# Sample's late products with cached keys, tied behind levels of linear attention, with their sums one step later

## The chip, the core and the metric

The program runs on one core of a Trainium2 chip. The metric is device time in microseconds of one execution, compared by the median of several. A core has a matmul engine (TensorE, in the profile PE; its weight loads are PEld), VectorE (DVE), ScalarE (ACT), GpSimd (POOL) and SyncE (SP), which here issues nearly all DMAs. Each engine works off its own queue in the order in which the program was built; an instruction that waits holds up all that stand behind it in its queue.

## What is computed

One inference step of a hybrid decoder layer, for a prompt of 2048 positions and for eight samples of eight new positions each. One projection is split into dilated sliding-window attention (8 heads of 64), gated linear attention (4 heads, key size 64, value size 128) and gates; both results are gated and go through one output projection.

```python
def reference(x_prompt, x_sample, cache_k_win, cache_v_win, state_gla, norm_w, w_in, ...):
    ...
        hp, kp, vp, st_p = mixer_layer(hp, pos_p, attend_prompt, s0, *params)
        att_s = functools.partial(attend_sample, cache_k_win[layer], cache_v_win[layer])
        hs, kn, vn, st_s = mixer_layer(hs, pos_s, att_s, state_gla[layer], *params)

def mixer_layer(x, pos, attend, s0, ...):
    z = rmsnorm(x, norm_w) @ w_in
    q, k, v, qb, kb, vb, g_lr, gate_a, gate_b = jnp.split(z, split_points(), axis=-1)
    ...
    o_a = attend(q, k, v)
    log_a = jax.nn.log_sigmoid(g_lr @ w_gate_up + b_gate) / GATE_TAU
    o_b, s_fin = gla_chunked(qb * DK_B ** -0.5, kb, vb, log_a, s0)
    ...

def dilated_branch_sample(q, k_buf, v_buf, window, dil):
    ...
    s = jnp.einsum('bthd,btnhd->bthn', q, kg) * (hd ** -0.5)
```

The change concerns the last line, the scores of a sample's queries with its cached keys, for the last two of the eight samples.

## The kernel before

The program is written out in full by Python code and put in order by a scheduler that keeps, on each engine, close to the order in which the code is written. Four phases follow each other: the first projections (q, k, v) with the prompt's first attention branches; the rest of the prompt's attention, woven with the projections of the linear attention's queries and keys; from about 736 us the prompt's linear attention, woven with the gate and value projections (`acc_g`, `acc_vb`, later `acc_gb`); and from about 1100 us the sample's attention with the output projection (`Y`).

**Linear attention** (class `gla_core`, `gla_prompt`) runs over eight blocks of 256 positions, called e0 to e7, each of two chunks of 128. Within a block the decays between positions are covered by seven levels, B = 1, 2, 4, ... 64. From the gates' projection `u` come `la` and, by a scan on VectorE, the running sums `b` (L223). Then for each level `front` (L229 on) forms on POOL the difference `D` (L236), on ScalarE its exponential `E` (L244, three instructions, two buffers), and on VectorE the scaled keys `ks` (L249) and queries `qbd` (L252). Two levels later `back` multiplies them on TensorE (`sc`, L280, and L266 for the last level) and VectorE copies the result by a mask into `Ac` (L286). In the first levels of a block the block before it is finished: `kd` on POOL, its transpose `ptk` (L323) copied by VectorE to `kdt` (L325), and in `chunk` the state update `U` (L1266), the output `O` (L1274, L1280) and the new state `Sbd` (L1287). The `U` of the second chunk reuses a buffer that the first chunk's `Sbd` reads.

**Products with cached keys** are steps of one sample b and one t of 0 to 7. `sample_keys` loads the query row, broadcast to all partitions (`qb`), and 128 keys of the branch with dilation 16 (`k3`), and for t under 4 those with dilation 4 (`k2`, used for t and t + 4). In the next step `sample_scores` calls `dot` twice: POOL multiplies (`pr`, L964), VectorE sums over each head (L965) into `sck`. The buffer `pr` is single, so POOL can begin a product only when VectorE has summed the one before. After t = 7 a DMA writes the scores out. The samples 0 to 5 are done beside the attention; samples 6 and 7, 16 steps with 32 products, stay for the third phase (`late_dots`).

**The weave** takes generators with a number of steps each and always advances the one whose share done is lowest. In the third phase these are the projections, the linear attention (74 steps, the first 15 empty), the fetch of a weight, and `late_dots` (33 steps: 15 empty, 17, and one). A generator may answer `WAIT`, and then the next is tried. What is left goes into a second weave with the sample's own linear attention (`sample_gla`), which begins when `late_dots` is done.

Of the kernel before, what the change touches and what calls it, by code (L numbers as in the profile page):

```python
# [7 lines left out]
F32 = mybir.dt.float32  # L8
# [5 lines left out]
ALU = mybir.AluOpType  # L14
# [4 lines left out]
P = 128  # L19
# [33 lines left out]
def tile_hymba(ctx: ExitStack, tc: tile.TileContext, A: dict):  # L53
    nc = tc.nc
    PE, ACT, DVE, POOL, SP = nc.tensor, nc.scalar, nc.vector, nc.gpsimd, nc.sync
# [87 lines left out]
    class gla_core:  # L143
# [85 lines left out]
        def front(self, li):  # L229
            gt, st, n, B = self.pools[1], self.st, self.n, self.levels[li]  # L230
            halves = lambda f: f.rearrange("p (m two B) -> p m two B", two=2, B=B)
            M = n // B
            bv = halves(self.b[:].rearrange("p a c -> p (a c)"))
            D = gt.tile([P, 2 * n], F32, name=f"D_{self.tagp}_{B}", tag="D", bufs=2)
            dv = halves(D[:])
            POOL.tensor_tensor(  # L236
                dv, bv, bv[:, :, 0:1, B - 1 : B].to_broadcast([P, M, 2, B]), ALU.subtract
            )
            E = st["E"][li % 2]
            ev = E[:, :, :n].rearrange("p i (m B) -> p i m B", B=B)  # L240
            for i, (rows, half) in enumerate(
                ((slice(0, P), 0), (slice(0, 64), 1), (slice(64, P), 1))
            ):
                ACT.activation(  # L244
                    ev[rows, i], dv[rows, :, half, :], AF.Exp, scale=(2 * half - 1) / 16.0
                )
            ks, qbd = st["ks"][li % 3], st["qbd"][li % 3]
            kv, qv = (halves(f.rearrange("p a c -> p (a c)")) for f in (self.kT, self.qT))
            DVE.tensor_tensor(  # L249
                halves(ks[:, : 2 * n])[:, :, 0, :], kv[:, :, 0, :], ev[:, 0], ALU.mult  # L250
            )
            DVE.tensor_tensor(  # L252
                qbd[:, :, :n].rearrange("p i (m B) -> p i m B", B=B),
                qv[:, :, 1, :].unsqueeze(1).to_broadcast([P, 2, M, B]), ev[:, 1:3], ALU.mult,
            )

        def back(self, li):
            st, n, C, nch, B = self.st, self.n, self.C, self.nch, self.levels[li]
# [96 lines left out]
    WAIT = object()  # L355
# [25 lines left out]
    with ExitStack() as c1:  # L381
# [579 lines left out]
        def dot(out, kt, qt, tag):  # L961
            sk = sk_state["pool"]
            pr = sk.tile([P, 512], F32, name=f"pr_{tag}", tag="pr", bufs=1)
            POOL.tensor_tensor(pr[:], kt, qt, ALU.mult)  # L964
            DVE.tensor_reduce(  # L965
                out, pr[:].rearrange("p (u k d) -> p u k d", u=2, k=4), AX.X, ALU.add
            )

        def sample_keys(b, t):
            sk = sk_state["pool"]  # L970
            qt = sk_state["q", t] = sk.tile([P, 512], F32, name=f"qb_{b}_{t}", tag="qbc")
            SP.dma_start(qt[:], q_s[8 * b + t : 8 * b + t + 1, :].to_broadcast([P, 512]))
            k3 = sk_state["k3", t] = sk.tile([P, 512], F32, name=f"k3_{b}_{t}", tag="k3")
            SP.dma_start(k3[:], ck[b].rearrange("(m r) c -> r m c", r=16)[t])
            if t < 4:
                k2 = sk_state["k2", t] = sk.tile([P, 512], F32, name=f"k2_{b}_{t}", tag="k2")
                SP.dma_start(k2[:], ck[b, W - 512 : W, :].rearrange("(j r) c -> r j c", r=4)[t])

        def sample_scores(b, t):
            if t == 0:  # L980
                sk_state["sc"] = sk_state["pool"].tile(
                    [P, 2, 64], F32, name=f"sck_{b}", tag="sc"
                )
            sc = sk_state["sc"]
            out = sc[:].rearrange("p g (u t k) -> p g t u k", u=2, t=8)[:, :, t]
            qt = sk_state["q", t]
            dot(out[:, 1], sk_state["k3", t][:], qt[:], f"3_{b}_{t}")
            dot(out[:, 0], sk_state["k2", t % 4][:], qt[:], f"2_{b}_{t}")
            if t == 7:
                SP.dma_start(sc_d[b * P : (b + 1) * P, :], sc[:].rearrange("p g c -> p (g c)"))  # L990

        def scores_of(batches):
            todo = [(b, t) for b in batches for t in (0, 4, 1, 5, 2, 6, 3, 7)]

            def step(i):
                if i < len(todo):
                    sample_keys(*todo[i])
                if i:
                    sample_scores(*todo[i - 1])

            return [lambda i=i: step(i) for i in range(len(todo) + 1)]
# [463 lines left out]
        c_sk = ExitStack()  # L1465

        def late_dots():
            for _ in range(15):
                yield
            sk_state["pool"] = c_sk.enter_context(  # L1470
                tc.tile_pool(name="sk3", bufs=2, reuse_waits="tile")
            )
            for f in scores_of(range(6, 8)):
                f()
                yield
            c_sk.close()
            mixed.add("dots")
# [3 lines left out]
                yield  # L1481

        gla_all = [chain(beginning(), gla_prompt()), 74]
        late = [late_dots(), 33]
        host = [rest("g", "vb"), steps("g") + steps("vb")]
        fetch = [load_w("gb"), 2 * KT + 1]
        left = weave(host, gla_all, fetch, late, until=[host, fetch])
# [506 lines left out]
```

## Time and profile before

| what | value |
|---|---|
| median of 3 runs | 1349.1 us |
| lowest and highest | 1347.7 and 1352.2 us |
| the profiled execution | 1350.2 us |
| its span, first to last instruction | 1348.4 us |
| mean granted clock of TensorE | 0.975 |
| DVE busy, 736 to 872 us and 872 to 957 us | 117.7 of 136 us and 52.9 of 85 us |
| POOL busy in the same | 100.6 and 44.8 us |
| PE busy in the same | 120.4 and 83.2 us |

A row of a group or of the timeline gives the line in the kernel, the engine, the operation, and what it writes and reads; the bracket behind a row of the timeline is the time for which the engine stood idle before it, and what ended that. Buffer and block numbers are left out of the names (`D_e` is `D` of any block). A busy TensorE may still run slowly: the granted clock is 1.00 or 0.50 in each slot.

### The profile page before, as it was taken

Reading aid. Unit: us, or ns where it says so; the run is one execution under the profiler, and the core shown is the slowest. Engines: PE = TensorE matmul, PEld = TensorE weight load, DVE = VectorE, ACT = ScalarE, POOL = GpSimd, SP = SyncE. Lnnn points to the kernel's source line nnn. Section 1 sums busy time; section 2 is a strip of 40 time slices with the busy share of each in tenths; the row PEclk is TensorE's granted clock in tenths of the full one; section 3 lists DMA queues with packets and bytes.
Section 4 is the critical chain, followed back from the end, with each engine's and each line's share of the span. In section 5 each row is a group of like instructions: output and inputs, shape, how many; then the busy total and the mean of one; then the engine's idle time right before and its main releaser. Section 6 shows DMA issues by size and latency. Waiting matters only on the chain.

```text
span 1348.4 us, 26203 instructions
## 1 busy us (share of the span) xinstructions
PE 1217.5 (90%) x8878; PEld 727.7 (54%) x8878; DVE 926.2 (69%) x2275; ACT 877.7 (65%) x2332; POOL 634.4 (47%) x598
## 2 busy tenths in 40 slices
PE   3797999888899889997989789999999979999998
PEld 1343565555566555676667556666554434444443
DVE  6366767788677966767665988755673388878741
ACT  5655787678568776878886656566764375556520
POOL 0086553778678645651114876744462133332310
PEclk9998999999999899999999999999999989999999
DMA  8859857767956699968986457543227579998752
GB/s 257 244 172 261 227 155 162 202 202 222 237 168 204 182 273 274 304 209 198 219 194 195 131 173 231 171 126 97 91 94 221 185 240 354 332 378 306 288 208 78
DMA packets 251800, 285.27 MB, mean 212 GB/s; under 512 B 125441, under 2 KB 160338, under 8 KB 251666
## 3 DMA queue, kind: packets, MB, share of 16 engines
q1 hardware_dynamic: 251666, 283.60, 70.0%
q8 instruction: 70, 1.15, 0.3%
q14 instruction: 64, 0.52, 0.1%
HBM read 183.12 MB, written 75.24 MB: 192 GB/s over the span
## 4 chain that ended last, share of the span: by engine, by line
PE 36%; DVE 17%; DMA 13%; POOL 12%; issue 12%; ACT 9%; SPq 2%; POOLq 0%; DVEq 0%; ACTq 0%
PE acc_qkb L1118 5%; PE Y L1616 4%; PE acc_g L1118 3%; PE acc_vb L1118 3%; POOL pr L964 3%; DVE qbd L252 3%; PE O L476 3%; PE s L443 3%; PE t L461 2%; PE acc_gb L1118 2%; DMA T_q<-qp_d 2%; PE acc_v L1118 2%; PE acc_k L1118 2%; PE acc_q L1118 2%; POOL pt L428 2%
## 5 line engine op out<-in xcount | busy, mean ns | idle before, releaser
L1118 PEld LDWEIGHTS <-hr 128*128 128x128 f16 x1824 | 175.3, 99 | 132.0 <-issue 14.0
L964 POOL TENSOR_TENSOR pr<-k,qb 128x512 f32<-128x512 f32 x128 | 177.0, 1383 | 117.3 <-DVE sck L965 80.8
L1118 PEld LDWEIGHTS <-hl 128*128 128x128 f16 x1248 | 122.1, 100 | 153.0 <-issue 25.3
L454 ACT ACTIVATE p<-p,o 128x256 f32<-128x256 f32 (+1 forms) x384 | 173.3, 455 | 45.7 <-DVE o L451 41.8
L1616 PE MATMUL Y<-w_o,mh 128*128 128x512 f16 x768 | 177.5, 381 | 3.6 <-ACT mh L1575 3.5
L428 POOL TENSOR_TENSOR pt<-p,pt 128x512 f16<-128x512 f32 (+1 forms) x80 | 94.7, 1184 | 158.6 <-ACT pt L427 137.9
L476 PE MATMUL O<-v,pt 128*128 128x128 f16 x1200 | 110.4, 221 | 27.0 <-POOL pt L428 8.7
L965 DVE TENSOR_REDUCE sck<-pr 128x8 f32<-128x512 f32 x128 | 87.1, 681 | 58.8 <-POOL pr L964 58.5
L1616 PEld LDWEIGHTS <-mh 128*128 128x128 f16 x768 | 71.9, 98 | 90.5 <-issue 8.7
L461 PE MATMUL t<-ident,p 128*128 128x128 f32 x600 | 106.2, 281 | 7.4 <-ACT p L454 3.0
L476 PEld LDWEIGHTS <-pt 128*128 128x128 f16 x1200 | 82.0, 98 | 51.8 <-POOL pt L428 14.1
L1658 POOL TENSOR_TENSOR tc<-oc,w 128x512 f32<-128x512 f32 x32 | 44.4, 1407 | 138.8 <-DVE w L1650 115.6
L1118 PE MATMUL acc_g<-w_g,hr 128*128 128x272 f16 (+1 forms) x768 | 104.0, 283 | 0.0
L1118 PE MATMUL acc_v<-w_v,hl 128*128 128x512 f16 x384 | 93.8, 388 | 8.3 <-DVE za L798 3.2
L244 ACT ACTIVATE E<-D_e 128x256 f32<-128x256 f32 x168 | 67.3, 418 | 49.3 <-POOL D_e L236 20.5
L1118 PE MATMUL acc_q<-w_q,hl 128*128 128x512 f16 x384 | 93.5, 393 | 5.6 <-ACT zs_k L676 4.2
L451 DVE CUSTOM_DVE_ANT_0 p<-s,m3w,scl_s 128x128 f32<-128x128 f32 (+1 forms) x256 | 89.0, 395 | 10.4 <-PE s L443 5.0
L1118 PE MATMUL acc_k<-w_k,hl 128*128 128x512 f16 x384 | 89.9, 379 | 2.1 <-ACT zs_k L676 1.6
L1118 PE MATMUL acc_vb<-w_vb,hr 128*128 128x512 f16 x384 | 90.8, 385 | 0.0
L443 PE MATMUL s<-kk,qq 128*128 128x256 f16 (+1 forms) x512 | 82.7, 273 | 6.9 <-DMA kk<-kp_d 3.6
L1118 PE MATMUL acc_gb<-w_gb,hr 128*128 128x512 f16 x384 | 87.1, 380 | 0.0
L461 PEld LDWEIGHTS t<-ident,p 128*128 128x128 f32 x600 | 68.4, 143 | 18.2 <-ACT p L454 7.7
(509 smaller groups left out, 2600.5 us busy)
## 6 DMA issues: line engine op xcount, KB each, us to landing
k<-in_cache_k_win SPq DMA_DIRECT2D x104, 256.0 KB
sv<-in_cache_v_win SPq DMA_DIRECT2D x24, 1024.0 KB
hr<-h_d SPq DMA_DIRECT2D x44, 512.0 KB
qb<-q_d SPq DMA_DIRECT2D x64, 256.0 KB
o_d<-o SPq DMA_DIRECT2D x96, 132.0 KB
oc<-o_d SPq DMA_DIRECT2D x48, 264.0 KB
x<-in_x_prompt SPq DMA_DIRECT2D x16, 512.0 KB
h_d<-hl SPq DMA_DIRECT2D x16, 512.0 KB
```

The costliest lines, as they stand in the source:

```text
L244: ACT.activation(ev[rows, i], dv[rows, :, half, :], AF.Exp, scale=(2 * half - 1) / 16.0)
L428: POOL.tensor_tensor(l, f, h, ALU.subtract)
L443: PE.matmul(s_ps[:, i * w : (i + 1) * w], q, k, start=(n == 0), stop=(n == len(prods) - 1),)
L451: DVE.tensor_tensor_reduce(s[:, sl], s_ps[:, sl], mask, neg, BIG, ALU.add, ALU.min, nmf(i))
L454: ACT.activation(s[:, sl], s[:, sl], AF.Exp, bias=nmf(i), scale=-1.0, accum_out=denf(i))
L461: PE.transpose(p_ps[:, i * P : (i + 1) * P], t["s"][:, i * P : (i + 1) * P], ident[:])
L476: PE.matmul(o_, t["pt"][:, c, (i * nb + b) * P : (i * nb + b + 1) * P], vf(i, b), start=(n == 0), stop=(n == 2 * nb - 1),)
L964: POOL.tensor_tensor(pr[:], kt, qt, ALU.mult)
L965: DVE.tensor_reduce(out, pr[:].rearrange("p (u k d) -> p u k d", u=2, k=4), AX.X, ALU.add)
L1118: PE.matmul(z, a_[:, k, :], w[:, p_, k, cols], start=(k == 0 and i == 0), stop=(k == KT - 1 and i == 2),)
L1616: PE.matmul(Y[:], a_[:, k, :], w_[:, part, k, :512], start=(i == 0), stop=(i == len(prods) - 1),)
L1658: eng.tensor_tensor(t_[:], oc[:, g, :, 0:64], w[:, g].unsqueeze(2).to_broadcast([P, NH, HD]), ALU.mult,)
```

## The change

`front` now keeps its `D` instruction and its `qbd` instruction in `st["pins"]`. `late_dots` starts after 6 empty steps and has 18 working steps in a weave of 25, so that it advances once for about three levels. In each step the sums of the step before last's keys, the loads of the next keys and the products of the last keys are issued, in this order, inside `tc.issue_after` for both pins: every POOL instruction of the step is queued behind that `D`, every VectorE instruction behind that `qbd`. A sum thus stands one step after its product. `pr` has four buffers of its own tags. `dot` is split, so that the summing (`sum_of`) and the writing out (`keep_scores`) can be called alone; samples 0 to 5 are computed as before.

```diff
--- before.py
+++ after.py
@@ -233,7 +233,7 @@
             bv = halves(self.b[:].rearrange("p a c -> p (a c)"))
             D = gt.tile([P, 2 * n], F32, name=f"D_{self.tagp}_{B}", tag="D", bufs=2)
             dv = halves(D[:])
-            POOL.tensor_tensor(
+            dec = POOL.tensor_tensor(
                 dv, bv, bv[:, :, 0:1, B - 1 : B].to_broadcast([P, M, 2, B]), ALU.subtract
             )
             E = st["E"][li % 2]
@@ -249,10 +249,11 @@
             DVE.tensor_tensor(
                 halves(ks[:, : 2 * n])[:, :, 0, :], kv[:, :, 0, :], ev[:, 0], ALU.mult
             )
-            DVE.tensor_tensor(
+            que = DVE.tensor_tensor(
                 qbd[:, :, :n].rearrange("p i (m B) -> p i m B", B=B),
                 qv[:, :, 1, :].unsqueeze(1).to_broadcast([P, 2, M, B]), ev[:, 1:3], ALU.mult,
             )
+            st["pins"] = (dec.ins, que.ins)
 
         def back(self, li):
             st, n, C, nch, B = self.st, self.n, self.C, self.nch, self.levels[li]
@@ -962,9 +963,17 @@
             sk = sk_state["pool"]
             pr = sk.tile([P, 512], F32, name=f"pr_{tag}", tag="pr", bufs=1)
             POOL.tensor_tensor(pr[:], kt, qt, ALU.mult)
+            sum_of(out, pr)
+
+        def sum_of(out, pr):
+
             DVE.tensor_reduce(
                 out, pr[:].rearrange("p (u k d) -> p u k d", u=2, k=4), AX.X, ALU.add
             )
+
+        def keep_scores(b, sc):
+
+            SP.dma_start(sc_d[b * P : (b + 1) * P, :], sc[:].rearrange("p g c -> p (g c)"))
 
         def sample_keys(b, t):
             sk = sk_state["pool"]
@@ -987,7 +996,7 @@
             dot(out[:, 1], sk_state["k3", t][:], qt[:], f"3_{b}_{t}")
             dot(out[:, 0], sk_state["k2", t % 4][:], qt[:], f"2_{b}_{t}")
             if t == 7:
-                SP.dma_start(sc_d[b * P : (b + 1) * P, :], sc[:].rearrange("p g c -> p (g c)"))
+                keep_scores(b, sc)
 
         def scores_of(batches):
             todo = [(b, t) for b in batches for t in (0, 4, 1, 5, 2, 6, 3, 7)]
@@ -1465,13 +1474,40 @@
         c_sk = ExitStack()
 
         def late_dots():
-            for _ in range(15):
+            for _ in range(6):
                 yield
+            scs = []
             sk_state["pool"] = c_sk.enter_context(
                 tc.tile_pool(name="sk3", bufs=2, reuse_waits="tile")
             )
-            for f in scores_of(range(6, 8)):
-                f()
+            todo = [(b, t) for b in range(6, 8) for t in (0, 4, 1, 5, 2, 6, 3, 7)]
+            prods, sums = [], []
+            for i in range(len(todo) + 2):
+                while "pins" not in st:
+                    yield WAIT
+                with ExitStack() as order:
+                    for p_ in st["pins"]:
+                        order.enter_context(tc.issue_after(p_))
+                    for out, pr in sums:
+                        sum_of(out, pr)
+                    if i > 1 and todo[i - 2][1] == 7:
+                        keep_scores(todo[i - 2][0], scs.pop(0))
+                    if i < len(todo):
+                        sample_keys(*todo[i])
+                    sums = []
+                    if 0 < i <= len(todo):
+                        b, t = todo[i - 1]
+                        if t == 0:
+                            scs.append(sk_state["pool"].tile(
+                                [P, 2, 64], F32, name=f"sck_{b}", tag="sc"
+                            ))
+                        out = scs[-1][:].rearrange("p g (u t k) -> p g t u k", u=2, t=8)[:, :, t]
+                        for g, k_ in ((1, sk_state["k3", t]), (0, sk_state["k2", t % 4])):
+                            pr = sk_state["pool"].tile(
+                                [P, 512], F32, name=f"pr{g}_{b}_{t}", tag="pr", bufs=4
+                            )
+                            POOL.tensor_tensor(pr[:], k_[:], sk_state["q", t][:], ALU.mult)
+                            sums.append((out[:, g], pr))
                 yield
             c_sk.close()
             mixed.add("dots")
@@ -1481,7 +1517,7 @@
                 yield
 
         gla_all = [chain(beginning(), gla_prompt()), 74]
-        late = [late_dots(), 33]
+        late = [late_dots(), 25]
         host = [rest("g", "vb"), steps("g") + steps("vb")]
         fetch = [load_w("gb"), 2 * KT + 1]
         left = weave(host, gla_all, fetch, late, until=[host, fetch])
```

What this makes of the queues, at three places (e0 to e5 in the names are the blocks; `pr_3_6_0` or `pr1_6_0` is the product of sample 6, t = 0, with the keys of dilation 16, `pr_2` or `pr0` with those of dilation 4).

POOL at the start of the linear attention, before:

```order
L177 TENSOR_TENSOR Ac_e1_10122<-ident64_83,dd_e1_10120 128x512
L964 TENSOR_TENSOR pr_3_6_0_10743<-k3_6_0_10650,qb_6_0_10648 128x512
L236 TENSOR_TENSOR D_e0_1_9937<-b_e0_9910 128x512
L236 TENSOR_TENSOR D_e0_2_9965<-b_e0_9910 128x512
L297 TENSOR_TENSOR qe_e0_10227<-kq_e0_9866,eb_e0_9913 128x512
L964 TENSOR_TENSOR pr_2_6_0_10746<-k2_6_0_10652,qb_6_0_10648 128x512
L236 TENSOR_TENSOR D_e0_4_9989<-b_e0_9910 128x512
```

and in the change:

```order
L177 TENSOR_TENSOR Ac_e1_10140<-ident64_83,dd_e1_10138 128x512
L236 TENSOR_TENSOR D_e0_1_9937<-b_e0_9910 128x512
L236 TENSOR_TENSOR D_e0_2_9974<-b_e0_9910 128x512
L298 TENSOR_TENSOR qe_e0_10257<-kq_e0_9866,eb_e0_9913 128x512
L236 TENSOR_TENSOR D_e0_4_9998<-b_e0_9910 128x512
L236 TENSOR_TENSOR D_e0_8_10035<-b_e0_9910 128x512
L1509 TENSOR_TENSOR pr1_6_0_10073<-k3_6_0_9958,qb_6_0_9956 128x512
L1509 TENSOR_TENSOR pr0_6_0_10075<-k2_6_0_9960,qb_6_0_9956 128x512
```

The first two products have moved from among the first `D`s of e0 to behind the fourth.

VectorE at the start of e4, before, from the scan `b` to the first new state:

```order
L223 SCALAR_TENSOR_TENSOR b_e4_11518<-scan_m_9438,la_e4_11513 128x256 x2
L325 COPY kdt_e3_11631<-ptk_e3_11626 128x512
L249 TENSOR_TENSOR ks0_9444<-kq_e4_11451,E0_9440 128x256
L252 TENSOR_TENSOR qbd0_9450<-kq_e4_11451,E0_9440 128x512
L249 TENSOR_TENSOR ks1_9446<-kq_e4_11451,E1_9442 128x128x2
L252 TENSOR_TENSOR qbd1_9452<-kq_e4_11451,E1_9442 128x512
L169 TENSOR_REDUCE dd_e5_11903<-prod_e5_11901 128x8
L249 TENSOR_TENSOR ks2_9448<-kq_e4_11451,E0_9440 128x64x4
L252 TENSOR_TENSOR qbd2_9454<-kq_e4_11451,E0_9440 128x512
L1287 SCALAR_TENSOR_TENSOR Sbd1_9458<-Sbd0_9456,eb_e3_11070,U_6_11673 64x128 x4
```

and in the change:

```order
L223 SCALAR_TENSOR_TENSOR b_e4_11552<-scan_m_9438,la_e4_11547 128x256 x2
L249 TENSOR_TENSOR ks0_9444<-kq_e4_11485,E0_9440 128x256
L252 TENSOR_TENSOR qbd0_9450<-kq_e4_11485,E0_9440 128x512
L970 TENSOR_REDUCE sck_7_11240<-pr1_7_1_11569 128x2x4
L970 TENSOR_REDUCE sck_7_11240<-pr0_7_1_11571 128x2x4
L326 COPY kdt_e3_11662<-ptk_e3_11657 128x512
L249 TENSOR_TENSOR ks1_9446<-kq_e4_11485,E1_9442 128x128x2
L252 TENSOR_TENSOR qbd1_9452<-kq_e4_11485,E1_9442 128x512
L169 TENSOR_REDUCE dd_e5_11923<-prod_e5_11921 128x8
L249 TENSOR_TENSOR ks2_9448<-kq_e4_11485,E0_9440 128x64x4
L252 TENSOR_TENSOR qbd2_9454<-kq_e4_11485,E0_9440 128x512
L1296 SCALAR_TENSOR_TENSOR Sbd1_9458<-Sbd0_9456,eb_e3_11112,U_6_11705 64x128 x4
```

Two sums have come in behind the first level's `qbd`, and `kdt` now stands behind them. e1, e2, e3 and e5 have two sums behind their first `qbd` as well; in e2 the copy `kdt` stood behind the second level's `ks` and `dd` before, and stands ahead of both now.

POOL at the same place, before:

```order
L315 TENSOR_TENSOR kd_e3_11553<-kd_e3_11553,kq_e3_11000 128x512
L1399 MEMSET qxs_0_13063 128x576
L1404 MEMSET S0_0_13066 128x2048
L236 TENSOR_TENSOR D_e4_1_11619<-b_e4_11518 128x512
L236 TENSOR_TENSOR D_e4_2_11666<-b_e4_11518 128x512
L167 TENSOR_TENSOR prod_e5_11901<-zqk_e5_11814 128x512
L236 TENSOR_TENSOR D_e4_4_11721<-b_e4_11518 128x512
```

and in the change:

```order
L316 TENSOR_TENSOR kd_e3_11597<-kd_e3_11597,kq_e3_11042 128x512
L236 TENSOR_TENSOR D_e4_1_11650<-b_e4_11552 128x512
L1509 TENSOR_TENSOR pr1_7_5_11682<-k3_7_5_11567,qb_7_5_11565 128x512
L1509 TENSOR_TENSOR pr0_7_5_11684<-k2_7_1_11406,qb_7_5_11565 128x512
L236 TENSOR_TENSOR D_e4_2_11698<-b_e4_11552 128x512
L167 TENSOR_TENSOR prod_e5_11921<-zqk_e5_11834 128x512
L236 TENSOR_TENSOR D_e4_4_11753<-b_e4_11552 128x512
```

Two products have come in between the first and the second `D`, and the two memsets of the sample's linear attention have moved away, to the end of e6. On SP the key loads and that attention's first loads move along with them, among the loads and stores of the projections.

## The prediction

> **What bounds the kernel now.** I read the page first, then the busy times by stretch, then the waits, then each engine in order of time around the waits, and last the granted clock in slots of 3.41 us. In the stretches the columns are the bounds in us, the length, and the busy time of PE, PEld, DVE, ACT and POOL (instructions in brackets), then clock, DMA share, GB/s.
>
> ```profile
> span 1348.4 us, 26203 instructions
> ...
> PE 1217.5 (90%) x8878; PEld 727.7 (54%) x8878; DVE 926.2 (69%) x2275; ACT 877.7 (65%) x2332; POOL 634.4 (47%) x598
> ```
> ```profile
> 736.00:872.00 136.00, 120.42 (x1058) 83.92 (x1056) 117.67 (x167) 82.47 (x216) 100.64 (x84) 0.95 0.59 184
> 872.00:957.00 85.00, 83.23 (x739) 58.17 (x738) 52.93 (x87) 54.57 (x146) 44.80 (x39) 1.00 0.34 105
> ...
> 1100.00:1348.00 248.00, 235.44 (x1704) 114.66 (x1704) 170.03 (x428) 117.39 (x185) 64.64 (x49) 0.99 0.78 279
> ```
>
> TensorE bounds the program: 90% of the span. What a change of order can win is TensorE's idle time and its time at a low clock. The change touches the stretch from 736 us, where the levels of linear attention begin, to about 957 us. In its first part, 736 to 872, TensorE idles 136.0 - 120.4 = 15.6 us and VectorE is busy 87% of the time; in the second part TensorE idles 1.8 us and VectorE is busy 62%. All 32 late products and sums stand in the first part:
>
> ```profile
> L964 POOL TENSOR_TENSOR pr<-k,qb 128x512 f32<-128x512 f32 x32 | 44.4, 1388 | 27.5 <-DVE sck L965 25.4 <-DMA k<-in_cache_k_win 2.0
> ...
> L965 DVE TENSOR_REDUCE sck<-pr 128x8 f32<-128x512 f32 x32 | 21.7, 678 | 11.8 <-POOL pr L964 11.6
> ```
>
> So the first part carries 21.7 us of VectorE's and 44.4 us of POOL's time that the second could carry. But that is not yet TensorE's time. These are the waits of TensorE that carry the sum (the bracket is its idle time before the row, and who ended it):
>
> ```profile
> 761.82 0.69 PE L280 MATMUL sc_e<-qbd,ks 128*64 128x64 f32 x16 [1.68 <-DVE Ac_e L286]
> ...
> 797.14 0.66 PE L323 MATMUL ptk_e<-ident,kd_e 128*128 128x128 f32 x4 [0.80 <-POOL kd_e L315]
> ...
> 804.96 0.66 PE L1266 MATMUL U<-vb,kdt_e 128*64 128x128 f32 x8 [2.47 <-DVE kdt_e L325]
> ```
> ```profile
> 850.20 0.66 PE L1266 MATMUL U<-vb,kdt_e 128*64 128x128 f32 x8 [2.42 <-DVE Sbd L1287]
> ```
>
> The first belongs to e0, the first of eight blocks of 256 positions, whose levels run from 739 us with little projection work between them; 2.47 and 2.42 stand where the levels of e2 and e3 start. There `U` needs `kdt` and then `Sbd` from VectorE, both queued behind the first levels. In the middle of a block, where most sums stand, TensorE hardly waits. **The place of a sum matters, not their number.**
>
> After three of these waits the clock halves (slots of 3.41 us; second figure PE busy, 0.50 or 1.00 the clock):
>
> ```profile
> 758.96:762.38 3.42, 1.25 (x32) 1.09 (x32) 3.42 (x7) 1.52 (x3) 1.86 (x2) 1.00 0.37 143
> 762.38:765.79 3.41, 3.41 (x20) 2.51 (x16) 3.31 (x5) 1.31 (x3) 1.79 (x3) 0.50 0.23 77
> ...
> 803.34:806.75 3.41, 1.29 (x10) 0.71 (x10) 3.41 (x6) 2.04 (x6) 3.41 (x4) 1.00 0.47 132
> 806.75:810.16 3.41, 3.11 (x12) 2.92 (x13) 3.37 (x8) 1.15 (x3) 3.41 (x4) 0.50 0.47 180
> 810.16:813.58 3.42, 3.42 (x29) 2.39 (x30) 2.41 (x8) 3.05 (x15) 3.23 (x4) 0.50 0.72 224
> ...
> 847.71:851.12 3.41, 0.99 (x15) 0.71 (x12) 3.25 (x7) 1.83 (x5) 3.41 (x4) 1.00 0.67 242
> 851.12:854.54 3.42, 3.42 (x14) 3.04 (x13) 3.38 (x5) 3.14 (x14) 3.42 (x3) 0.50 0.74 235
> ...
> 994.48:997.89 3.41, 2.17 (x13) 1.82 (x14) 3.28 (x9) 1.55 (x4) 1.83 (x3) 1.00 0.00 0
> ```
>
> A slot with 1.25, 1.29 or 0.99 us of TensorE work is followed by half clock, one with 2.17 is not. Four slots at half clock cost up to 4 x 3.41 / 2 = 6.8 us.
>
> **The change, part by part.** Nothing is removed: 32 products and 32 sums before and after. They become 16 steps, three in each of blocks e1 to e5 (behind levels 1, 8 and 64) and one in e0, and a sum stands one step after its product.
>
> *Start of e0.* Before, the first `D` of e0 queues on POOL behind a product that waits for its keys:
>
> ```profile
> 738.22 1.26 POOL L964 TENSOR_TENSOR pr<-k,qb 128x512 f32<-128x512 f32 x1 [2.00 <-DMA k<-in_cache_k_win]
> 739.44 2.04 POOL L236 TENSOR_TENSOR D_e<-b_e 128x512 f32<-128x512 f32 x2
> ```
> ```profile
> 735.72 1.62 DVE L223 TENSOR_TENSOR_SCAN b_e<-scan_m,la_e 128x256 f32<-128x256 f32 x2
> ```
> ```profile
> 738.03 0.69 ACT L745 ACTIVATE vbs<-acc_vb,wi_vb 128x512 f32<-128x512 f32 x1
> 740.51 1.22 ACT L244 ACTIVATE E<-D_e 128x256 f32<-128x256 f32 x3 [1.79 <-POOL D_e L236]
> ```
>
> Its input `b` is ready at 737.34. In the change `D` comes first, so `E` starts when ACT is free at 738.72: **-1.8 us**. TensorE idles in e0, so the chain behind `E` is what it waits for; the product's wait is then late for nothing, since products follow only behind level 8.
>
> *Rest of e0 and e1.* The order moves one sum (0.68) out of e0's levels, and the product ahead of the second `kd` of e1 (the 0.80 wait at 797.14) goes. Bounds 0 and -2.5; I take **-1.5**, the two rows added.
>
> *Starts of e2 and e3.* In e2 `kdt` stood behind two instructions that are now behind it, and two sums come ahead of it:
>
> ```profile
> 794.96 3.27 DVE L223 TENSOR_TENSOR_SCAN b_e<-scan_m,la_e 128x256 f32<-128x256 f32 x2
> ...
> 802.23 1.48 DVE L249 TENSOR_TENSOR ks<-kq_e,E 128x256 f32<-128x256 f32 x1
> 803.63 0.67 DVE L169 TENSOR_REDUCE dd_e<-prod_e 128x8 f32<-128x512 f32 x1
> ```
> ```profile
> 907.30 2.03 DVE L223 TENSOR_TENSOR_SCAN b_e<-scan_m,la_e 128x256 f32<-128x256 f32 x2
> ...
> 918.69 1.47 DVE L1287 SCALAR_TENSOR_TENSOR Sbd<-Sbd,eb_e,U 64x128 f32<-64x128 f32 x4
> ```
>
> 1.48 + 0.67 - 2 x 0.68 = 0.8 us earlier. The scan before it took 3.27 with products on POOL beside it and 2.03 in e5 with none; the change has none there: 1.2 earlier. Together -2.0 of the 2.47. In e3 as many sums stand ahead of `Sbd` as before (two), so the 2.42 stays. **-2.0**; bounds -4.9 (both waits closed) and +0.7 (a sum more in e3).
>
> *Starts of e4 and e5.* They had no sums and get two each, ahead of `kdt` and so of `Sbd`. TensorE comes to the `U` that needs `Sbd` here:
>
> ```profile
> 920.93 0.61 PE L1266 MATMUL U<-vb,kdt_e 128*64 128x128 f32 x8
> ```
>
> `Sbd` ended at 918.69 + 1.47 = 920.16, so 0.8 us of cover. Two sums are 1.36: 0.6 us over. Two products (2 x 1.39) also stand between the first and second `D`, which delays the second level's `E`; as that level's `ks` already waits behind the sums, I count half of one product, 0.7. That is 1.3 per start, **+2.7** for two; bounds 0 and +6.7 (sums and products wholly exposed, less the cover: 1.36 + 2.78 - 0.8 in each).
>
> *Products elsewhere.* Beside levels 8 and 64 they stand where VectorE and POOL have room. With one buffer POOL waited 25.4 us for sums; with four and a step between it shouldn't. Cover: the scans of e2 and e5 end at 798.2 and 909.3, so a block is 37 us and a step some 12, where a late key load cost POOL 2.0 us at 738. If that cover fails, a `D` waits behind a product as at 738. The queue of SP issues the keys a step ahead of the product, past the tile loads, whose buffers are four.
>
> *Sample's linear attention.* Its first memsets and loads (POOL and SP) move from the start of e4 to the end of e6. TensorE's order there doesn't move. I take 0, and keep +1 as the upper end.
>
> *Clock.* Of the four slots the one at 762 and the two at 806 should go (1.7 each, -5.1) and one come back at e4 or e5 (+1.7): **-3.4**; bounds -6.8 and +3.4. The Trainium skill, "TensorE: Matmul & The Clock Gate", Part 1, has the clock fall only after about a whole idle window of 3.4 us. This trace disagrees: the slots above fell after 1.0 to 1.3 us of work in the window. By the page closing waits of 2.5 us would win no clock, and the sum would be -2.6 instead of -6.0.
>
> Sum: -1.8 - 1.5 - 2.0 + 2.7 - 3.4 = **-6.0 us**. The profiled execution took 1350.2 us (span 1348.4, 1.8 around it), 1.1 above the median of 1349.1; so 1344.2 against itself, 1343 against the median.
>
> **The rivals.**
> - *Given back at the starts.* The sums stand ahead of `kdt` in every block: what e0 wins (3.3) is lost at e2 to e5, and the clock falls as often as now. For it: VectorE's queue is strict and `kdt` is short of cover everywhere. -3.3 - 2.0 + 5.4 (twice the 2.7) is about nothing: 1349 against the median, 1345 to 1353.
> - *Slower starts.* One mechanism, at the second `U` of e2 to e5: each of the four starts waits as long as e2 and e3 do now, 2.45 us, two of them anew: +4.9; and each pulls the clock down for two slots as at 806: eight slots for four, +6.8; less 3.3 won in e0: +8.4, so 1357. It decides when a wait leaves under about 1.3 us of work in a slot.
> - *The clock stays.* Halvings come, but not from these waits: the sum without the clock term, 1346.5. Against it: all three follow the emptiest slots. This is the page's rule above.
> - *The last stage gives it back.* From 1100 us on the change's order differs too, though nothing was edited there; TensorE idles 12.6 us of 248. A third or half more of that is +4 to +6 and takes the gain away: 1347 to 1349.
> - *It doesn't do what it says.* The order shows that it does; what it can't show is a late key load, which I count under the first rival.
>
> **How the numbers follow.** Forecast 0.47 (1336 to 1345), given back 0.27, slower starts 0.17, clock stays 0.04, last stage 0.05. About 4 us (0.3%) is what a measurement can tell from no change. Faster by more: the forecast, and a little of the first rival, 0.48. Slower by more: slower starts and the worst of the last stage, 0.19. Within: 0.33. The range adds the good ends (-1.8 - 2.5 - 4.9 - 6.8 = -16, about 1333) and reaches up to the slower starts at 1357.
>
> **What would show it.** The first `E` of e0 some 1.8 us after `b` instead of 3.2; the wait before `U` in e2 under 1 us; waits of 1 to 1.5 us before the second `U` in e4 and e5; POOL's wait for sums near zero; two fewer half-clock slots or more between 736 and 957. Wrong it would be if e4 and e5 wait over 2 us with the clock down behind them, if a product waits for its keys ahead of a `D`, or if the stretch from 1100 us changes by more than 4 us.

## The result and the profile after

The changed kernel takes 1339.9 us (median of four runs, 1337.1 to 1341.6) beside 1350.7 for the kernel before on the same chip. The ratio is 0.9911, with a 95% interval of 0.9883 to 0.9940: 12 us faster, between 8 and 16 (by the two medians alone 10.8). The profiled execution took 1341.1 us against 1350.2, so its rows account for 9.1 of them. Its page, and the three stretches as before (bounds, length, busy PE, PEld, DVE, ACT, POOL, then clock, DMA share, GB/s):

```profile
span 1339.3 us, 26206 instructions
...
PE 1215.7 (91%) x8878; PEld 726.8 (54%) x8878; DVE 924.8 (69%) x2275; ACT 876.6 (65%) x2332; POOL 635.4 (47%) x598
```
```profile
736.00:872.00 136.00, 127.39 (x1123) 87.08 (x1122) 115.67 (x166) 87.84 (x228) 98.14 (x79) 0.97 0.57 179
872.00:957.00 85.00, 82.49 (x734) 57.21 (x732) 63.45 (x100) 54.50 (x155) 51.66 (x45) 1.00 0.42 128
...
1100.00:1348.00 248.00, 227.76 (x1665) 110.13 (x1663) 163.16 (x416) 113.04 (x179) 59.19 (x45) 1.00 0.74 271
```

TensorE does the same work. In the first stretch it idles 136.0 - 127.4 = 8.6 us instead of 15.6, in the second 2.5 instead of 1.8. VectorE and POOL are hardly less busy in the first stretch, since more of the program now fits into it (1123 matmuls of TensorE instead of 1058). The groups of the late products and sums, 736 to 1021 us:

```profile
L1509 POOL TENSOR_TENSOR pr<-k,qb 128x512 f32<-128x512 f32 x32 | 47.1, 1490 | 1.2 <-DVE sck L970 1.2
L970 DVE TENSOR_REDUCE sck<-pr 128x8 f32<-128x512 f32 x32 | 20.3, 673 | 0.0
```

POOL's wait for sums went from 25.4 us to 1.2. The start of e0, in the timeline of VectorE, POOL and ACT, and the scan of `b` in e7:

```profile
736.54 1.62 DVE L223 TENSOR_TENSOR_SCAN b_e<-scan_m,la_e 128x256 f32<-128x256 f32 x2
...
973.51 1.27 DVE L223 TENSOR_TENSOR_SCAN b_e<-scan_m,la_e 128x256 f32<-128x256 f32 x2
```
```profile
738.24 2.04 POOL L236 TENSOR_TENSOR D_e<-b_e 128x512 f32<-128x512 f32 x2 [1.21 <-DVE b_e L223]
```
```profile
739.35 2.46 ACT L244 ACTIVATE E<-D_e 128x256 f32<-128x256 f32 x6
```

`D` follows `b` at once and `E` starts 1.2 us after it (before: 3.2). The waits of TensorE that answer to those of before, in its timeline:

```profile
762.03 1.39 PE L267 MATMUL sc_e<-qbd,ks 128*64 128x128 f32 x8 [2.10 <-DVE Ac_e L287]
...
814.20 2.29 PE L1127 MATMUL acc_vb<-w_vb,hr 128*128 128x512 f16 x5 [2.35 <-ACT zg L733]
...
842.21 0.66 PE L1275 MATMUL U<-vb,kdt_e 128*64 128x128 f32 x8 [0.77 <-DVE Sbd L1296]
...
877.17 0.66 PE L1275 MATMUL U<-vb,kdt_e 128*64 128x128 f32 x8 [0.42 <-DVE Sbd L1296]
...
912.22 0.66 PE L1275 MATMUL U<-vb,kdt_e 128*64 128x128 f32 x8 [0.77 <-DVE Sbd L1296]
```

The wait of 2.47 before the first `U` of e2 is gone; a new one of 2.35 stands later in e2, for ACT. In e3 to e5 the second `U` waits 0.77, 0.42 and 0.77 us. The granted clock in slots, each with the one ahead of it:

```profile
759.26:762.68 3.42, 1.32 (x12) 0.98 (x11) 3.32 (x6) 1.51 (x5) 3.42 (x4) 1.00 0.49 156
762.68:766.09 3.41, 3.41 (x18) 2.12 (x15) 3.41 (x5) 3.34 (x7) 3.41 (x3) 0.50 0.22 77
810.47:813.88 3.41, 1.38 (x19) 1.08 (x16) 3.35 (x5) 3.33 (x11) 2.96 (x3) 1.00 0.56 154
813.88:817.29 3.41, 3.09 (x8) 1.13 (x8) 3.38 (x5) 2.58 (x13) 1.43 (x1) 0.50 0.49 149
984.55:987.96 3.41, 1.50 (x8) 1.17 (x9) 3.34 (x8) 1.93 (x4) 1.82 (x2) 1.00 0.34 130
987.96:991.37 3.41, 3.41 (x23) 3.01 (x23) 2.22 (x5) 1.54 (x5) 1.32 (x2) 0.50 0.21 77
```

Two half-clock slots up to 957 us instead of four, and one more in e7. The one at 762 has stayed.

So the account closes on TensorE. The scan of `b` in e7 before:

```profile
982.77 1.27 DVE L223 TENSOR_TENSOR_SCAN b_e<-scan_m,la_e 128x256 f32<-128x256 f32 x2
```

From the scan of `b` in e0 to that in e7 the kernel before took 982.77 - 735.72 = 247.0 us, the changed one 973.51 - 736.54 = 237.0. Of these 10.0 us, idle time of TensorE is 17.4 - 11.1 = 6.3 (by blocks: e0 and e1 8.7 to 4.9, e2 4.1 to 2.9, e3 2.8 to 0.8, e4 to e6 1.8 to 2.5; all counted from scan to scan) and clock 2 x 1.7 = 3.4. Behind e7 nothing more is won: the end comes 9.1 us earlier, e7's scan 9.3.

### The profile page after: what moved, and what is told of

Its sections match the earlier page's. It is cut to its first block, busy times and chain, and to the rows that moved or that the text cites. A ratio compares the mean times of both kernels' runs of the same rounds, so it can differ in the third digit from the quotient of the medians.

```text
span 1339.3 us, 26206 instructions
## 1 busy us (share of the span) xinstructions
PE 1215.7 (91%) x8878; PEld 726.8 (54%) x8878; DVE 924.8 (69%) x2275; ACT 876.6 (65%) x2332; POOL 635.4 (47%) x598
## 4 chain that ended last, share of the span: by engine, by line
PE 38%; DVE 18%; DMA 16%; POOL 9%; issue 9%; ACT 8%; SPq 2%; POOLq 0%; DVEq 0%; ACTq 0%
PE Y L1652 4%; PE acc_qkb L1127 3%; PE acc_vb L1127 3%; PE acc_v L1127 3%; PE acc_g L1127 3%; PE acc_gb L1127 3%; PE O L477 3%; PE t L462 3%; PE s L444 3%; DVE qbd L252 3%; PE acc_q L1127 2%; DMA T_q<-qp_d 2%; POOL pr L965 2%; PE acc_k L1127 2%; DMA sv<-in_cache_v_win 2%
## 5 line engine op out<-in xcount | busy, mean ns | idle before, releaser
L1127 PEld LDWEIGHTS <-hr 128*128 128x128 f16 x1824 | 174.5, 99 | 134.3 <-issue 17.4
L965 POOL TENSOR_TENSOR pr<-k,qb 128x512 f32<-128x512 f32 x96 | 132.5, 1381 | 91.2 <-DVE sck L970 57.1
L477 PEld LDWEIGHTS <-pt 128*128 128x128 f16 x1200 | 82.5, 99 | 51.2 <-POOL pt L429 14.1
L452 DVE CUSTOM_DVE_ANT_0 p<-s,m3w,scl_s 128x128 f32<-128x128 f32 (+1 forms) x256 | 88.9, 394 | 11.6 <-PE s L444 6.2
```

The lines of the kernel that those rows point to most:

```text
L452: DVE.tensor_tensor_reduce(s[:, sl], s_ps[:, sl], mask, neg, BIG, ALU.add, ALU.min, nmf(i))
L477: PE.matmul(o_, t["pt"][:, c, (i * nb + b) * P : (i * nb + b + 1) * P], vf(i, b), start=(n == 0), stop=(n == 2 * nb - 1),)
L1127: PE.matmul(z, a_[:, k, :], w[:, p_, k, cols], start=(k == 0 and i == 0), stop=(k == KT - 1 and i == 2),)
```

## Experiments

The runs are called e1 to e12; a run is always written "run e4", and a bare e4 is the block. Three things can have made the gain: the **place** (two ordering constraints hold each step behind the `D` and `qbd` of a level), the **density** (16 steps spread over e0 to e5 instead of e0 to e3), and **buffers and delay**. All runs in one table, the ratio of each to runs of the kernel before on the same chip. The third column is the time from the scan of e0 to that of e7 in the profiled execution, the last two TensorE's idle time and its half-clock slots within it. These three come from one execution each, by the records of its trace. (The profiled execution of run e9 was 10.7 us above its median; its e0 began at 743.1 us, in the changed kernel at 736.5, and the column leaves that out.)

| kernel | ratio to before (95%) | e0 to e7, us | idle | slots |
|---|---|---|---|---|
| before | 1 | 247.0 | 17.4 | 4 |
| changed | 0.9911 (0.9883-0.9940) | 237.0 | 11.1 | 2 |
| run e1: no late products or sums | 0.9893 (0.9868-0.9917) | 232.3 | 7.7 | 1 |
| run e2: before, four buffers | 1.0000 (0.9982-1.0018) | 247.3 | 18.6 | 5 |
| run e3: changed, no constraints | 1.0017 (0.9997-1.0037) | 249.6 | 19.8 | 6 |
| run e4: changed, steps in e0 to e3 | 0.9979 (0.9961-0.9997) | 247.6 | 19.0 | 4 |
| run e5: before, no sums | 0.9979 (0.9958-1.0000) | 247.7 | 15.7 | 6 |
| run e6: before, no products | 0.9924 (0.9902-0.9947) | 234.7 | 12.6 | 1 |
| run e7: changed, steps in e1 to e5 | 0.9939 (0.9914-0.9964) | 241.2 | 13.2 | 3 |
| run e8: changed, behind levels 4 to 32 | 0.9953 (0.9935-0.9972) | 242.3 | 14.7 | 2 |
| run e9: run e4 with copies for products | 0.9918 (0.9890-0.9947) | 236.8 | 11.0 | 2 |
| run e10: changed, products on VectorE | 0.9934 (0.9917-0.9951) | 237.3 | 11.7 | 0 |
| run e11: changed, two buffers | 0.9913 (0.9893-0.9933) | 237.1 | 9.8 | 3 |
| run e12: changed, sums at once | 0.9925 (0.9910-0.9940) | 237.7 | 12.5 | 1 |

**Run e1, the floor.**

```diff
-    POOL.tensor_tensor(pr[:], k_[:], sk_state["q", t][:], ALU.mult)
-    sums.append((out[:, g], pr))
+    if t == 0 and g: DVE.memset(scs[-1][:], 0.0)
```

> The changed kernel with all 32 late products and sums left out: the scores of sample's batches 6 and 7 against cached keys are zeros, and every load stays. This is the floor of any placing of them. Theory A (density: the gain came because fewer products and sums stand in blocks e0 and e1, and where they stand now they are nearly free): 1337 to 1340 us, no more than 3 us under the changed kernel's 1340. Theory B (the starts of e2 to e5 still pay for sums ahead of kdt and Sbd, 0.4 to 0.8 us each, and the clock with them): 1330 to 1335.

The 32 products and sums cost the kernel before 0.0107 x 1351 = 14.5 us and the changed one some 2.5; the two intervals overlap, so anything from nothing to about 7 is possible (an estimate from their widths). The median of 1336.6 lies between the two forecasts and nearer the first: where they now stand they cost little. In the profiled pair 4.7 us of e0 to e7 are left.

**Runs e2 and e3, buffers without place, and place taken away.**

```diff
 # run e2, on the kernel before
-    pr = sk.tile([P, 512], F32, name=f"pr_{tag}", tag="pr", bufs=1)
+    pr = sk.tile([P, 512], F32, name=f"pr_{tag}", tag="pr",
+                 bufs=1 if sk is sk_first else 4)
 # run e3, on the changed kernel
-    for p_ in st["pins"]:
-        order.enter_context(tc.issue_after(p_))
```

> The kernel before with four product buffers for the late products, nothing else: products and sums keep their program order. Theory C (one buffer made POOL and VectorE wait for each other, 25.4 us of POOL's waits, and D behind those): most of the gain, 1341 to 1344 us. Theory A (density in e0 and e1): no gain, since the products only run earlier and stand ahead of D as before or more so: 1350 to 1356. Theory D (place, that is, products kept behind the first instructions of a level): the same as A here.

> The changed kernel without the two ordering constraints per step; four buffers, sums a step later and the spread of the steps in the program stay, but the instructions now go where they are ready, that is, into e0 to e2 ahead of D. Theory C (buffers and delayed sums): keeps the gain, 1340 to 1343 us. Theories A and D: the gain is gone, 1349 to 1356, with D of e0 again behind products that wait for keys.

Four buffers alone win nothing. But the order did not stay as it was: in POOL's queue 24 of the 32 products now stand ahead of the first `D` of e2 (before 13), so run e2 has more density as well, and only run e11 below tells of the buffers by themselves. Without the constraints the whole gain is gone, with buffers, delay and the written spread kept. Why shows in POOL's timeline of run e3, where `b` of e0 was ready at 745.2 (its scan, 742.50, took 2.68 us beside the products, before 1.62):

```profile
740.59 2.65 POOL L1507 TENSOR_TENSOR pr<-k,qb 128x512 f32<-128x512 f32 x2 [0.64 <-DMA k<-in_cache_k_win]
743.20 1.43 POOL L177 TENSOR_TENSOR Ac_e<-ident,dd_e 128x512 f32<-128x512 f32 x1
744.59 2.88 POOL L1507 TENSOR_TENSOR pr<-k,qb 128x512 f32<-128x512 f32 x2
747.43 2.04 POOL L236 TENSOR_TENSOR D_e<-b_e 128x512 f32<-128x512 f32 x2
```

Free to move, four products stand ahead of the first `D`, which comes 2.2 us after `b`, and all 32 stand ahead of e3. The constraints are what makes the spread happen; as it takes away place and spread together, this run can't tell the two apart.

**Run e4, constraints without spread.**

```diff
-    for _ in range(6):
+    for _ in range(10):
...
-    late = [late_dots(), 25]
+    late = [late_dots(), 42]
```

> The changed kernel with the 16 steps in e0 to e3 instead of e0 to e5 (ten empty turns for six, 42 parts for 25): constraints, four buffers and delayed sums stay. Theory A (density): most of the gain is lost, 1346 to 1351 us, and e0 and e1 take again about 59 us from scan to scan of e2. Theory D (place) and C (buffers): the gain stays, 1339 to 1343.

Of 12 us it keeps 2.8 (0.4 to 5.3), with every step still held behind a `D` and a `qbd`; from the scan of e0 to that of e2 it takes 59.1 us, as foretold (changed 51.9). Two of TensorE's waits in e1 tell where much of the rest went:

```profile
757.69 0.69 PE L281 MATMUL sc_e<-qbd,ks 128*64 128x64 f32 x16 [2.69 <-DVE qbd L252]
760.56 1.12 PE L281 MATMUL sc_e<-qbd,ks 128*64 128x64 f32 x16 [2.18 <-DVE qbd L252]
```

The first `D` of e0 again follows `b` at once (POOL 736.48, `b` done at 736.4) and e0's idle time falls to 1.4 us, but e1, with twelve products against six, idles 8.0 us (with six in the changed kernel 2.1, with nine before 5.5, without any 2.2). All five waits between the scans of e1 and e2 are for `sc_e`, that is, for `qbd` or `Ac` of some level (the two shown for e0's last levels, by the order on VectorE), and none for `kdt` or `Sbd` at the start: here the number of steps counts. In e2 and e3 run e4 does not keep the place in the sense of the prediction, since six and four sums stand ahead of `Sbd` there (two in the changed kernel), and the second `U` of e3 waits 2.6 us. What e0 wins, the blocks behind it give back.

**Runs e5 and e6, which half of the late work costs.**

```diff
 # run e5: late products without their sums
+    if sk is sk_first:
         DVE.tensor_reduce(out, pr[:]..., AX.X, ALU.add)
 # run e6: late sums without their products
+    if sk is sk_first:
         POOL.tensor_tensor(pr[:], kt, qt, ALU.mult)
+    else: pr = kt
```

> The kernel before without the late sums: the 32 products stay on POOL, the scores of batches 6 and 7 are zeros. All of the late work together costs the kernel before about 1351 - 1337 = 14 us (by the kernel without scores). Theory A1 (VectorE's own time in e0 and e1 is what density costs: 21.7 us of sums on an engine busy 87%): most of the 14 us go with the sums, 1337 to 1342. Theory A2 (products cost through POOL: a D stands behind each, and VectorE's qbd takes 1400 ns beside them against 684 ns without): they stay with the products, 1344 to 1350.

> The counterpart: the kernel before without the late products; the 32 sums stay on VectorE with the same shape, but add up the loaded keys, so the scores of batches 6 and 7 are other numbers. Theory A1 (VectorE's own time): 1345 to 1350 us. Theory A2 (products through POOL): 1336 to 1341, and qbd falls from 1162 ns to about 700 in the stretch from 736 to 960 us.

Without the sums 2.8 us are won (0 to 5.7), without the products 10.3 (7.2 to 13.2). The median of run e6, 1343.1, lies between the two forecasts, and all of its 32 sums have moved up ahead of e2, since no product holds them up; so this is the price of the products together with that order. The groups of the kernel before and of run e6 (736 to 960 us):

```profile
L236 POOL TENSOR_TENSOR D_e<-b_e 128x512 f32<-128x512 f32 x49 | 59.2, 1222 | 9.6 <-DVE b_e L223 5.2 <-ACT E L244 4.1
...
L252 DVE TENSOR_TENSOR qbd<-kq_e,E 128x512 f32<-128x512 f32 x47 | 54.6, 1162 | 0.4 <-ACT E L244 0.4
```
```profile
L236 POOL TENSOR_TENSOR D_e<-b_e 128x512 f32<-128x512 f32 x49 | 58.5, 1207 | 28.8 <-DVE b_e L223 17.1 <-ACT E L244 11.3
...
L252 DVE TENSOR_TENSOR qbd<-kq_e,E 128x512 f32<-128x512 f32 x47 | 48.7, 1037 | 0.1
```

POOL now waits 28.8 us ahead of `D` (9.6 in the kernel before): `D` more often runs as soon as its input is there. `qbd` fell only from 1162 to 1037 ns, since it runs beside `D` as well; I had expected 700.

**Runs e9 and e10, how a product costs.**

```diff
 # run e9, on run e4
-    POOL.tensor_tensor(pr[:], k_[:], sk_state["q", t][:], ALU.mult)
+    POOL.tensor_copy(pr[:], k_[:])
 # run e10, on the changed kernel
-    POOL.tensor_tensor(pr[:], k_[:], sk_state["q", t][:], ALU.mult)
+    DVE.tensor_tensor(pr[:], k_[:], sk_state["q", t][:], ALU.mult)
```

> The kernel with the 16 steps in e0 to e3, with every product replaced by a POOL copy of the keys (one tensor read instead of two; the scores of batches 6 and 7 are other numbers). The steps stay in e0 to e3, nearly in the same order. A copy of this size is estimated at 0.94 us from the 472 ns of one of half the size, against 1.44 for the product. Theory G (a product costs because VectorE's two-input operations take over twice as long beside it): qbd beside copies takes about 0.7 us instead of 1.7, and 1337 to 1341 us. Theory H (it costs because D stands behind it in POOL's queue): two thirds of POOL's time stay, so most of the cost does, 1343 to 1347 us, whatever qbd takes.

> The changed kernel with the 32 late products on VectorE instead of POOL, at the same steps; everything is computed. An estimate for one product is 0.68 us, as for qbd alone, so 22 us more on VectorE and 47 us less on POOL, and fewer qbd of 1.7 us. Theory G or H (products cost through POOL): as fast as the changed kernel or faster, 1336 to 1340 us, near the kernel without scores. Theory A1 (VectorE's own time counts as much): slower, 1342 to 1347.

```profile
L1509 POOL COPY pr<-k 128x512 f32<-128x512 f32 x32 | 22.4, 715 | 12.9 <-DVE sck L970 9.8 <-DMA k<-in_cache_k_win 3.1
```
```profile
L1509 DVE TENSOR_TENSOR pr<-k,qb 128x512 f32<-128x512 f32 x32 | 30.7, 998 | 0.0
```

In run e9 (first group) the cost of density is nearly gone with the steps left in e0 to e3. But the copy took 715 ns, half of a product and not the two thirds that I had estimated, so both theories would see at least half of the cost go; the time (1336 to 1343 by the ratio's interval) lies on the first one's side without excluding the second. Nor is the spread quite that of run e4: ten products and eight sums in e1, not twelve of each. The run also shows that the move of the sample's memsets is not the gain: here they begin at 865 us (before 873, in the changed kernel 918), and the kernel is as fast as the changed one within the interval.

Between contention and queue the trace of run e4 says more. Its e1 and e2, from scan to scan (the columns as in the stretches above, VectorE being the third):

```profile
752.22:793.86 41.64, 33.63 (x318) 24.66 (x317) 39.94 (x54) 23.07 (x64) 35.87 (x29) 0.92 0.58 184
793.86:834.74 40.88, 35.78 (x299) 24.54 (x297) 40.56 (x63) 25.60 (x66) 33.20 (x25) 0.96 0.69 215
```

VectorE is busy 80.5 of 82.5 us, and its only wait of more than 0.15 us there is for TensorE. If a `D` that is late behind products held the levels up, VectorE would have to wait for `E`, and no such wait is there. So in these two blocks VectorE's own time is used up: by 26 sums, and by `ks` and `qbd`, which take 1.03 and 1.28 us in the mean (in e1 and e2 of the changed kernel, with 14 sums, 0.69 and 1.24, and VectorE is busy 62.8 of 71.3 us). In the same blocks of run e5, which has no sums, VectorE does wait for `E`, 6.2 us; there the queue has a share.

In run e10 the products took 998 ns on VectorE, not 680, and 31 us more on VectorE cost no more than the interval can tell from the changed kernel: spread out, the products are cheap on either engine, and moving them off POOL wins nothing further.

**Runs e7 and e8, other spreads.**

```diff
 # run e7
-    for _ in range(6):
+    for _ in range(15):
-    late = [late_dots(), 25]
+    late = [late_dots(), 34]
 # run e8
+    st["level"] = li      # behind st["pins"] = ...
-    while "pins" not in st:
+    while "pins" not in st or st["level"] not in (2, 3, 4, 5):
```

> The changed kernel with fifteen empty turns and 34 parts: the steps begin behind the last level of e1 and end in e5; e0 has none, e2 to e5 have three or four each. Theory A (density in e0 and e1 is what costs, and late steps are nearly free): as fast as the changed kernel or faster, 1336 to 1341 us. Theory E (what counts is the number of steps in any one block: three are free, four are not): slower than the changed kernel, 1342 to 1346.

> The changed kernel with steps allowed only behind levels 4 to 32 of a block, never behind 1, 2 or 64: no sum stands ahead of kdt or of Sbd, but two steps meet behind level 16. Theory F (what is left, 3 us over the kernel without scores, is paid at the starts of e2 to e5): 1336 to 1339 us, and the waits before the second U of e3, e4 and e5 (0.77, 0.42, 0.77 us) are gone. Theory E (steps that meet in one place cost more): 1342 to 1347.

Neither beats the changed kernel. Their medians, 1342.8 and 1344.7, are those of theory E, but both intervals overlap that of the changed kernel. Run e7 leaves e0 empty and puts eight products into each of e2, e3 and e4; the second `U` of e3, e4 and e5 waits 0.97, 1.18 and 1.92 us. In run e8 four products stand together behind level 16, and four sums stand together behind level 4 of the next block, ahead of its `Sbd`; here those of e4, in the timeline of VectorE and of TensorE:

```profile
874.19 2.45 DVE L971 TENSOR_REDUCE sck<-pr 128x8 f32<-128x512 f32 x4
876.56 1.47 DVE L1297 SCALAR_TENSOR_TENSOR Sbd<-Sbd,eb_e,U 64x128 f32<-64x128 f32 x4
```
```profile
878.09 0.66 PE L1276 MATMUL U<-vb,kdt_e 128*64 128x128 f32 x8 [1.56 <-DVE Sbd L1297]
```

I had expected these waits to vanish. But a sum behind level 4 still stands ahead of `Sbd`. Two sums more there made 1.56 out of 0.42: 1.1 us for two sums of 0.6 to 0.7. That fits a price of nearly the whole sum at this place, once the cover is used up.

**Runs e11 and e12, buffers and delay.**

```diff
 # run e11
-    tag="pr", bufs=4
+    tag="pr", bufs=2
 # run e12
-    sums.append((out[:, g], pr))
+    sum_of(out[:, g], pr)
```

> The changed kernel with two product buffers instead of four. With sums a step later a product must wait for the sum of the step before, which moves it in POOL's order: out of the starts of most blocks, up to four together behind the last level. If the four buffers carry a share of the gain: 1343 to 1349 us. If spread is all: 1338 to 1342, and POOL waits for sums a few us in all instead of 1.2.

> The changed kernel with each sum in the step of its product instead of a step later; four buffers, constraints and spread stay. If the delay carries a share (VectorE waits for the product at the head of its queue): 1343 to 1347 us, and VectorE's idle time before sums is over 5 us. If spread is all: 1338 to 1342.

```profile
L1509 POOL TENSOR_TENSOR pr<-k,qb 128x512 f32<-128x512 f32 x32 | 44.2, 1398 | 35.9 <-DVE sck L970 35.9
```

With two buffers POOL waits 35.9 us for sums, more than the kernel before and far more than the few that I had expected, and the time is that of the changed kernel. With the sums in the step of their product it is the same within the interval. So neither the four buffers nor the delayed sums carry a share that can be measured, and POOL's 25.4 us of waits were no cause: with the spread kept, 35.9 us of them cost nothing that can be measured.

## Why the prediction was right, by its steps

The direction and the time were right (forecast 1343, 1340 measured), and the signs of most terms; the reason in one sentence was not. The gain was forecast too small: 6.0 us against 9.1 in the profiled pair and 12 by the ratio. In the profiled pair the clock term came as forecast, and TensorE's idle time up to e7 fell by 6.3 us where the terms make 2.6; 2.1 of the difference lie in e4 and e5, 1.2 in e2 and e3, 0.5 in e0 and e1.

- **Start of e0** (-1.8): `E` starts 1.2 us after `b` instead of 3.2, so -2.0. Right for `E`. TensorE's own idle time in e0 fell only from 3.2 to 2.8; without any late work it is 2.5 (run e1). The gain shows in e1, where e0's last levels run (5.5 to 2.1). Run e4 has this start too and gives the gain back in e1.
- **Rest of e0 and e1** (-1.5): TensorE's idle time of e0 and e1 fell by 3.8; with the first term I had 3.3, of which the 0.80 at 797.14 stands in e2 by the scans. Near in size. That TensorE hardly waits in the middle of a block was too short a reading of the trace before: besides the wait that I showed, three of 1.5 to 1.8 us stand in e0's levels and three of 0.5 to 0.7 in e1, and the latter three, which are gone, make half of what was won here.
- **Starts of e2 and e3** (-2.0): -3.2 in idle time, otherwise distributed. The 2.47 in e2 is gone as foretold, but 1.2 is all that e2 wins, since TensorE comes to wait for ACT's `zg` at 814. In e3 I let the 2.42 stay because as many sums stand ahead of `Sbd`; it fell to 0.77. From scan to the end of `Sbd` VectorE takes no less than before (836.18 to 850.14, now 827.64 to 842.15), so fewer sums are not the reason. But TensorE comes to that `U` 13.8 us after the scan instead of 11.6: VectorE's chain is further ahead of it. I had read the wait as a property of the block; in this pair it is a lag carried in from the blocks ahead.
- **Starts of e4 and e5** (+2.7): the waits at the second `U` are 0.42 and 0.77, together 1.2, or +0.6 against the idle time of e4 and e5 before. This is the term that was mis-sized. What was measured, 0.6 at each start in the mean, is the size of the two sums beyond the cover; the half product of 0.7 that I added to each does not show.
- **Products elsewhere** (0): POOL's wait for sums 1.2 us, no product waits for its keys. Right within what run e1 can tell; but the four buffers, which I thought to be the cover, weren't needed (run e11).
- **Clock** (-3.4): four slots became two, -3.4 to 957 us; one more in e7 gives 1.7 back. The number is right by luck, for other slots went than I had named. I let the one at 762 go, and it stayed; the two at 806 went, but one came at 814 behind the new wait for ACT; the one at 851, which I had kept, went with e3's wait; and none came in e4 or e5. The slots ahead of the three held 1.32, 1.38 and 1.50 us of TensorE's work, not none, so the rival by which only an empty window lowers the clock has this trace against it, as that of before.
- **The last stage** neither gave nor took: of 248.0 - 227.8 = 20.2 us without TensorE in the stretch from 1100 us, 8.7 lie behind the program's end at 1339.3, which leaves 11.5. As the stretch now begins later in the program, the last 248 us ahead of each end compare better: 13.2 us without TensorE, before 13.0.

The rivals: *given back at the starts* and *slower starts* fell, since the starts of e4 and e5 cost 1.2 us and no clock. The mechanism itself exists, as run e8 shows with two sums more ahead of `Sbd`.

The step that failed is the sentence "The place of a sum matters, not their number." Run e4 kept the constraints and raised the number per block, and 9 of 12 us were lost, in e1 by waits for the levels themselves and not at the start; by runs e5 and e6 the products, which I had priced at nothing outside e0, e1 and the starts, cost the kernel before 10.3 of the 14.5 us, and the sums 2.8. Shown is that holding the steps behind a level is not enough without the spread, that the spread does not come without the constraints, and that buffers and delay carry no share that can be measured. By what path ten or twelve products in a block cost is shown for e1 and e2 of run e4 alone: there it is VectorE's own time, with the sums and the longer `ks` and `qbd`, and not a late `D`. What share the queue of POOL has in the kernel before is not settled.

## What to carry to other kernels

Side work on a shared engine is cheap as long as each block's chain of levels still ends before TensorE needs it, and its price grows faster than its amount. With 22 products in e0 to e3 (changed) TensorE idles 8.6 us there and with none 6.5 (run e1), but with all 32 from 15.6 to 18.6 (before, runs e2, e3 and e4; one execution each). So spread it evenly and hold it there with constraints, because a scheduler that puts instructions where they are ready will pull it together again. A long wait on an engine off the path is by itself no price: ask what stands behind the waiting instruction. And read a wait at the start of a block together with the lag carried in from the block ahead, not from what its own queue holds alone.

## What the runs showed of the hardware

- VectorE's `qbd` (two tensors of SBUF) takes 0.68 us with POOL idle, and in the changed kernel a mean of 1.70 beside a late product and 1.59 beside POOL's other work (17 and 16 instances of 49 between 736 and 960 us). In 32 of these 33 it ended about 0.55 us behind the end of a POOL instruction that ran beside it; the last ran beside a memset, which reads nothing, and took 0.67. Beside the copies of run e9 it is 0.99 (8 instances). The sums, which read one tensor, took 0.67 to 0.68 each in the changed kernel, whatever POOL did. The Trainium skill, "SBUF — State Buffer", section "SBUF: two separate sides", has a VectorE instruction with two SBUF inputs and a GpSimd instruction that reads SBUF exclude each other for a whole instruction; of VectorE's other instructions it names only those in a 2-port mode. These rows agree.
- The mean `qbd` of the changed kernel is longer than before (1332 against 1162 ns, both from 736 to 960 us), although the kernel is faster: a longer `qbd` is by itself no price, as long as TensorE doesn't wait for VectorE's chain.
